# Where eight modulation columns of the hybrid block's gate are worked out: five at the end of the first branch, three later

## The chip, the cores and the metric

The kernel runs on one core of a Trainium2 chip. The metric is the time of one execution on the device in microseconds (us), as the median of several executions. A core has five engines with a queue each: TensorE (PE) for matmuls, with its weight loads shown apart (PEld), VectorE (DVE) and ScalarE (ACT) for elementwise work, GpSimd (POOL), and SyncE (SP), which here issues the large transfers from memory. Each engine works its own instructions off in the order in which they were written into its queue, and waits at an instruction until the results that it needs are there.

## What is computed

Two layers work on 256 tokens of width 1024. Each layer has three branches in a row: a gated feed-forward branch, a mixer and another feed-forward branch. In layer 0 the mixer is a hybrid (a recurrence and a state-space part), in layer 1 an mLSTM. So there are six branches, numbered 0 to 5 below; branch 0 is the first feed-forward branch, branch 1 the hybrid. Each branch is modulated by a vector `c`, by three sets of 1024 numbers: a shift, a scale and a gate.

```python
mod = (c_act @ ada_w[layer] + ada_b[layer]).reshape(bsz, N_SUB, 3, D_MODEL)[:, :, :, None, :]

def modulate(t, sub):
    return rms_norm(t, norm_g[layer, sub]) * (1.0 + mod[:, sub, 1]) + mod[:, sub, 0]

h = modulate(x, 0)
x = x + HALF_STEP * (1.0 + mod[:, 0, 2]) * swiglu(h, ffn_w_gate[layer, 0], ffn_w_up[layer, 0], ffn_w_down[layer, 0])
h = modulate(x, 1)
...
x = x + (1.0 + mod[:, 1, 2]) * y.astype(x.dtype)
```

The change is about `mod[:, 1, 2]` of layer 0, the gate of the hybrid: it is needed only when the hybrid's output projection ends.

## The kernel before

**Layout.** Features lie on the 128 partitions, tokens along the row. `x` is 8 chunks of 128 by 256. A weight matrix is cut into tiles of 128 by 128, and all tiles of the program stand in one stream in memory in the order of their use. Eight tiles are a piece (512 KB); there are 366 pieces, 66 of them in branch 0 (pieces 0 to 65) and 54 in branch 1 (pieces 66 to 119). Products are made in a split form: a weight and an activation are each a high part and a low part, and one tile costs three matmuls (L372 high by high, L373 high by low, L374 low by high).

**A piece on its way.** SP issues its transfer into `wraw` (four buffers, L91), ACT makes the high part `whi` (L99), DVE the low part `wlo` (L100). Four buffers mean that the transfer of piece n+4 waits for the low part of piece n. The parts have six buffers.

**The modulation.** A branch needs 24 columns of 128 numbers: 8 of shift, 8 of scale, 8 of gate. One column is one job: a transfer of 512 KB (L228, three buffers, on SP's queue among the pieces) and one DVE instruction that multiplies by `c` and sums (L230, tile `ada`). A table says at which pieces the jobs of a range are issued, in equal steps:

```python
for s, (lo, hi), jobs in ADA_PLAN:
    for i, b in enumerate(jobs):
        due.setdefault(starts[s] + lo + (hi - lo) * i // len(jobs), []).append(b)
```

Job b belongs to branch b // 24; jobs 40 to 47 are the gate of the hybrid, 48 to 63 shift and scale of branch 2. A planner in the framework then works out, from its own costs, in what order each engine's instructions stand; so a change of the table also moves other instructions of DVE, ACT, PE and SP against each other.

**From branch 0 to branch 1.** Branch 0 ends with its down projection: eight outputs `od` of 22 tiles. After each, DVE adds it to `x` (L492), ACT squares it (L349), DVE sums the squares (L353) and ACT and DVE make a scaled copy `hb` (L418, L419). `begin` (L422) starts branch 1: PE multiplies the first four output tiles `bc` with these copies, which don't need the norm yet. Meanwhile PE sums the squares over the partitions (`rst_n`, L317), DVE works the reciprocal root out in eight dependent instructions on 128 by 2 numbers (L329, then L283 to L292, tiles `rsv_n`, `rsy_n`, `rsw_n`), PE spreads it (`rsb_n`, L340), ACT copies it (`rs`, L427), and then each of the 8 chunks gets its normed input: a product `ht` (L402, DVE), its high part (L404, ACT) and its low part (L405, DVE, written into `hb`). After that the four `bc` are finished (`bct`, L451, and `shc_bc`, L453, DVE).

**The hybrid's first products.** `xbc` 0 to 7 are eight outputs of one piece each, with `dtT` (24 small matmuls) among them. They stand in four PSUM banks that are used in turn, so `xbc4` takes the bank of `xbc0`. A bank comes free when its convolution has read it: one ACT instruction (L619) and three DVE instructions (L622, on 255, 254 and 253 columns). The four `bc` go through twelve such L622 too (`ssd`).

**Later in the hybrid** come the products `xl`, `z` and `ri` with the recurrence's elementwise work, then the state-space part: ACT makes exponentials `mt` (L875), DVE masks them (L877), PE multiplies (`y`, L897); after that the output projection, whose inputs `ysb` are split on ACT and DVE (L359, L360).

Of the kernel before, what the change touches and what calls it, by code (L numbers as in the profile page):

```python
# [37 lines left out]
for _n, _w in COLS:  # L38
# [25 lines left out]


ADA_PLAN = [
    (0, (17, 43), range(16, 40)), (0, (43, 65), range(48, 64)), (1, (22, 37), range(40, 48)),
    (2, (6, 60), range(64, 104)), (3, (6, 60), range(104, 136)), (5, (6, 40), range(136, 144)),
]

# [1348 lines left out]
```

## Time and profile before

| | |
|---|---|
| median of 3 executions | 1103.49 us (1103.45 to 1104.76) |
| the profiled execution | 1104.36 us, of which the span of its instructions is 1102.6 us |
| PE busy | 1088.9 us (99%) |
| DVE busy | 920.0 us (83%) |
| ACT busy | 641.7 us (58%) |
| memory read | 269.77 MB, 246 GB/s over the span |

Times in the profile are us from the start of the span. A row of the timeline has the start, the duration, the engine, the line, the operation, what it writes and reads, the shape, how many equal ones follow each other, and in brackets how long the engine sat idle before it and who ended that. Matmuls overlap each other: each is shown as 0.28 us long, but the next starts 0.113 us later when nothing is in the way, so a gap between two starts tells of a wait even where PE counts as busy. Two DVE instructions overlap as well, by about 0.08 us.

### The profile page before, as it was taken

What the parts mean: (1) busy time and instruction counts of PE and PEld (TensorE: products, weight loads), DVE (VectorE), ACT (ScalarE), POOL (GpSimd) and SP (SyncE); (2) the same over time, 40 slices, a digit from 0 to 9 for tenths busy, and PEclk for the clock granted to TensorE, in tenths of its full rate; (3) what the DMA queues carried; (4) which work ended last, traced back from release to release, by engine and by line L of the source; (5) the groups of instructions that cost most, each with busy time, mean ns of one, the idle gap of its engine ahead of it and who ended that gap; (6) DMA issues with size and microseconds to landing.
All of it is one profiled execution on the core that took longest, in us unless ns stands there. A gap on an engine that the chain in (4) does not pass through costs nothing.

```text
span 1102.6 us, 23366 instructions
## 1 busy us (share of the span) xinstructions
PE 1088.9 (99%) x9350; PEld 1074.5 (97%) x9350; DVE 920.0 (83%) x1651; ACT 641.7 (58%) x1051; POOL 9.4 (1%) x29
## 2 busy tenths in 40 slices
PE   8999999999999999999999999999999999999997
PEld 6999999999999999999999999999999999999997
DVE  7999989899999899989699988869778868766552
ACT  5665545578986565454554554548776655544452
POOL 0000000000000000000000000010000000000000
PEclk9999999999999999999999999999999999999999
DMA  9899999565855489999848998953422554776551
GB/s 371 333 328 372 382 343 353 185 209 182 279 167 175 144 294 371 352 354 329 281 163 317 333 331 307 312 203 116 147 94 95 200 192 161 263 238 198 193 173 39
DMA packets 74990, 272.34 MB, mean 247 GB/s; under 512 B 8417, under 2 KB 8577, under 8 KB 74882
## 3 DMA queue, kind: packets, MB, share of 16 engines
q1 hardware_dynamic: 74304, 269.49, 69.4%
q8 instruction: 73, 1.20, 0.4%
q0 software_dynamic: 432, 1.10, 0.4%
q14 instruction: 35, 0.29, 0.1%
q10 hardware_dynamic: 146, 0.27, 0.1%
HBM read 269.77 MB, written 1.05 MB: 246 GB/s over the span
## 4 chain that ended last, share of the span: by engine, by line
PE 90%; DVE 5%; ACT 2%; DMA 1%; issue 1%; SPq 0%; DVEq 0%; ACTq 0%
PE gu L373 13%; PE gu L374 13%; PE gu L372 13%; PE od L373 10%; PE od L372 10%; PE od L374 10%; DVE wlo L100 2%; PE zz L373 1%; PE zz L374 1%; PE zz L372 1%; PE gu_f L434 1%; PE gu_f L436 1%; PE gu_f L435 1%; DVE xc L622 1%; DVE ada L230 1%
## 5 line engine op out<-in xcount | busy, mean ns | idle before, releaser
L100 DVE TENSOR_TENSOR wlo<-wraw,whi 128x1024 fp32r<-128x1024 f32 x366 | 445.6, 1222 | 94.7 <-ACT whi L99 93.2
L99 ACT CAST whi<-wraw 128x1024 fp32r<-128x1024 f32 x364 | 379.5, 1050 | 222.5 <-PE od L373 70.9
L373 PE MATMUL gu<-hb,whi 128*128 128x256 f32 x1312 | 361.0, 276 | 1.3 <-DVE hb L569 1.3
L374 PE MATMUL gu<-hb,wlo 128*128 128x256 f32 x1312 | 360.6, 276 | 0.0
L372 PE MATMUL gu<-hb,whi 128*128 128x256 f32 x1312 | 357.8, 277 | 1.6 <-ACT hb L404 1.0
L373 PEld LDWEIGHTS gu<-hb,whi 128*128 128x128 f32 x1312 | 246.3, 188 | 1.9 <-DVE hb L569 1.9
L372 PEld LDWEIGHTS gu<-hb,whi 128*128 128x128 f32 x1312 | 244.2, 188 | 2.5 <-ACT hb L404 1.2
L374 PEld LDWEIGHTS gu<-hb,wlo 128*128 128x128 f32 x1312 | 246.3, 188 | 0.0
L372 PE MATMUL od<-ph,whi 128*128 128x256 f32 x704 | 194.3, 276 | 0.0
L373 PE MATMUL od<-ph,whi 128*128 128x256 f32 x704 | 194.3, 276 | 0.0
L374 PE MATMUL od<-ph,wlo 128*128 128x256 f32 x704 | 194.3, 276 | 0.0
L230 DVE SCALAR_TENSOR_TENSOR ada<-ada,cact 128x1024 f32<-128x1024 f32 x144 | 175.4, 1220 | 0.9 <-DMA ada<-in_adaT_dram 0.9
L372 PEld LDWEIGHTS od<-ph,whi 128*128 128x128 f32 x704 | 132.2, 188 | 0.0
L373 PEld LDWEIGHTS od<-ph,whi 128*128 128x128 f32 x704 | 132.2, 188 | 0.0
L374 PEld LDWEIGHTS od<-ph,wlo 128*128 128x128 f32 x704 | 132.2, 188 | 0.0
L359 ACT CAST ph<-fg 128x256 fp32r<-128x256 f32 x88 | 35.4, 410 | 102.0 <-DVE fg L516 101.9
L360 DVE TENSOR_TENSOR ph<-fg,ph 128x256 fp32r<-128x256 f32 x88 | 36.7, 423 | 12.3 <-ACT ph L359 12.1
L492 DVE SCALAR_TENSOR_TENSOR x<-od,gate,x 128x256 f32<-128x256 f32 x48 | 23.1, 482 | 27.5 <-PE od L374 27.5
L349 ACT ACTIVATE sq_o<-x 128x256 f32<-128x256 f32 x42 | 17.6, 419 | 41.7 <-DVE x L492 37.6
L373 PE MATMUL zz<-hb,whi 128*128 128x256 f32 x128 | 36.3, 284 | 0.0
L372 PE MATMUL zz<-hb,whi 128*128 128x256 f32 x128 | 36.2, 283 | 0.0
L374 PE MATMUL zz<-hb,wlo 128*128 128x256 f32 x128 | 36.2, 283 | 0.0
(412 smaller groups left out, 1953.2 us busy)
## 6 DMA issues: line engine op xcount, KB each, us to landing
wraw<-in_wst_dram SPq DMA_DIRECT2D x366, 512.0 KB, 4.6
ada<-in_adaT_dram SPq DMA_DIRECT2D x144, 512.0 KB, 5.6
xn<-in_x_dram SPq DMA_DIRECT2D x2, 512.0 KB, 4.1
wgr<-in_ml_wg_dram POOLq DMA_DIRECT2D x3, 256.0 KB, 3.0
out_dram<-res SPq DMA_DIRECT2D x3, 256.0 KB, 2.4
out_dram<-res ACTq DMA_DIRECT2D x1, 256.0 KB, 2.8
cols<-in_cols_dram SPq DMA_DIRECT2D x1, 226.0 KB, 7.3
wkr<-in_ml_wkr_dram POOLq DMA_DIRECT2D x1, 128.0 KB, 2.3
```

The lines of the kernel that those rows point to most:

```text
L99: raw_hi = nc.scalar.copy(hi, raw)
L100: self.last = nc.vector.tensor_tensor(out=lo, in0=raw, in1=hi.bitcast(F32), op=ALU.subtract)
L230: return nc.vector.scalar_tensor_tensor(out=raw, in0=raw, scalar=1.0, in1=cact, op0=ALU.mult, op1=ALU.mult, accum_out=mods[s][:, m:m + 1])
L349: square = nc.scalar.activation(q, x, AF.Square).ins
L359: nc.scalar.copy(hi, src)
L360: nc.vector.tensor_tensor(out=both[:, 1, :], in0=src, in1=hi.bitcast(F32), op=ALU.subtract)
L372: m = nc.tensor.matmul(dst, wh, both[:, 0, :], start=start, stop=False, skip_group_check=True)
L373: nc.tensor.matmul(dst, wh, both[:, 1, :], start=False, stop=False, skip_group_check=True)
L374: nc.tensor.matmul(dst, wl, both[:, 0, :], start=False, stop=stop, skip_group_check=True)
L434: nc.tensor.matmul(dst, wh, rh, start=(k == 0), stop=False)
L435: nc.tensor.matmul(dst, wh, rl, start=False, stop=False)
L492: nc.vector.scalar_tensor_tensor(out=xs_t[d], in0=dst, scalar=g[:, d:d + 1], in1=xs_t[d], op0=ALU.mult, op1=ALU.add)
```

## The change

Only the table changes. Jobs 40 to 44, five columns of the hybrid's gate, are issued after jobs 48 to 63 in branch 0, over pieces 43 to 65, where 16 jobs stood over pieces 43 to 64; so there are 21 jobs over 23 pieces. Jobs 45 to 47 are issued in the hybrid over 12 pieces (24 to 35), where eight jobs stood over 15 (22 to 36). Nothing is added to the work and nothing is taken from it.

```diff
@@ -64,7 +64,7 @@
 ADA_PLAN = [
-    (0, (17, 43), range(16, 40)), (0, (43, 65), range(48, 64)), (1, (22, 37), range(40, 48)),
+    (0, (17, 43), range(16, 40)), (0, (43, 66), [*range(48, 64), *range(40, 45)]), (1, (24, 36), range(45, 48)),
     (2, (6, 60), range(64, 104)), (3, (6, 60), range(104, 136)), (5, (6, 40), range(136, 144)),
 ]
```

The planner orders the engines' queues anew. Three places of DVE's queue follow. The first is where branch 0 ends: the last addition to `x` (`od_7`) and the start of the reciprocal root. Before:

```order
L492 SCALAR_TENSOR_TENSOR x<-od_7_2555,gate_1962,x 128x256
L720 TENSOR_SCALAR dt<-cols 128x8
L329 TENSOR_SCALAR rsv_n_2667<-rst_n_2662 128x2
L419 SCALAR_TENSOR_TENSOR hb<-x,scale_1968,hb 128x256
L283 TENSOR_SCALAR rsy_n_2670<-rsv_n_2667 128x2
```

And now:

```order
L492 SCALAR_TENSOR_TENSOR x<-od_7_2567,gate_1965,x 128x256
L720 TENSOR_SCALAR dt<-cols 128x8
L100 TENSOR_TENSOR wlo_2549<-wraw_2546,whi_2548 128x1024
L230 SCALAR_TENSOR_TENSOR ada_2552,mod_1184<-ada_2552,cact 128x1024
L419 SCALAR_TENSOR_TENSOR hb<-x,scale_1971,hb 128x256
L329 TENSOR_SCALAR rsv_n_2682<-rst_n_2677 128x2
```

The low part of piece 67 and one of the moved columns now stand between the last addition and the root. The second place follows at once: the rest of the root, up to the first normed chunk `ht_0`. Before:

```order
L286 TENSOR_TENSOR rsw_n_2669<-rsy_n_2670 128x2
L287 SCALAR_TENSOR_TENSOR rsw_n_2669<-rsw_n_2669,rsv_n_2667 128x2
L288 SCALAR_TENSOR_TENSOR rsw_n_2669<-rsw_n_2669 128x2
L289 SCALAR_TENSOR_TENSOR rsy_n_2670<-rsw_n_2669,rsy_n_2670 128x2
L290 TENSOR_TENSOR rsw_n_2669<-rsy_n_2670 128x2
L291 SCALAR_TENSOR_TENSOR rsw_n_2669<-rsw_n_2669,rsv_n_2667 128x2
L292 SCALAR_TENSOR_TENSOR rsy_n_2670<-rsw_n_2669,rsy_n_2670 128x2
L100 TENSOR_TENSOR wlo_2690<-wraw_2687,whi_2689 128x1024
L402 SCALAR_TENSOR_TENSOR ht_0_2807<-x,scale_1968,rs_2661 128x256
```

And now:

```order
L286 TENSOR_TENSOR rsw_n_2684<-rsy_n_2685 128x2
L100 TENSOR_TENSOR wlo_2589<-wraw_2586,whi_2588 128x1024
L230 SCALAR_TENSOR_TENSOR ada_2592,mod_1184<-ada_2592,cact 128x1024
L287 SCALAR_TENSOR_TENSOR rsw_n_2684<-rsw_n_2684,rsv_n_2682 128x2
L288 SCALAR_TENSOR_TENSOR rsw_n_2684<-rsw_n_2684 128x2
L289 SCALAR_TENSOR_TENSOR rsy_n_2685<-rsw_n_2684,rsy_n_2685 128x2
L290 TENSOR_TENSOR rsw_n_2684<-rsy_n_2685 128x2
L291 SCALAR_TENSOR_TENSOR rsw_n_2684<-rsw_n_2684,rsv_n_2682 128x2
L292 SCALAR_TENSOR_TENSOR rsy_n_2685<-rsw_n_2684,rsy_n_2685 128x2
L100 TENSOR_TENSOR wlo_2622<-wraw_2619,whi_2621 128x1024
L100 TENSOR_TENSOR wlo_2705<-wraw_2702,whi_2704 128x1024
L402 SCALAR_TENSOR_TENSOR ht_0_2822<-x,scale_1971,rs_2676 128x256
```

The low part of piece 68 and the last of the five moved columns stand inside the root, and the low parts of pieces 69 and 70 behind it; before, only that of piece 70 stood there, and those of 67 to 69 ahead of the last addition. From `ht_0` to the convolutions of `xbc0` the same instructions stand in another order (the four `bct` come earlier, the first `bct` behind `ht_1`). On PE, `dtT` now stands among the products of `xbc0` and `xbc1`, and the spread of the root ten tiles later; between `xbc3` and `xbc4` nothing was put. The third place is in the state-space part, ahead of the first mask `mt` (L877). Before:

```order
L100 TENSOR_TENSOR wlo_4090<-wraw_4087,whi_4089 128x1024
L819 SCALAR_TENSOR_TENSOR lru_aq<-a_7_4012,lru_aq 128x256
L230 SCALAR_TENSOR_TENSOR ada_4093,mod_1184<-ada_4093,cact 128x1024
L939 TENSOR_SCALAR lru_aq<-lru_aq 128x1024
L881 TENSOR_TENSOR ce_4022<-ce_4022,ssd_2656 128x512
L939 TENSOR_SCALAR lru_aq<-lru_aq 128x1024
L877 TENSOR_TENSOR mt_4021<-mt_4021,cbt 128x1024
```

And now:

```order
L100 TENSOR_TENSOR wlo_4096<-wraw_4093,whi_4095 128x1024
L812 SCALAR_TENSOR_TENSOR lru_x<-thi_4013,lru_x 128x256
L819 SCALAR_TENSOR_TENSOR lru_aq<-a_7_4018,lru_aq 128x256
L939 TENSOR_SCALAR lru_aq<-lru_aq 128x1024
L881 TENSOR_TENSOR ce_4028<-ce_4028,ssd_2671 128x512
L877 TENSOR_TENSOR mt_4027<-mt_4027,cbt 128x1024
```

Of six columns that stood ahead of this mask in the hybrid, two are left; a third stands behind it.

## The prediction

> **What bounds the kernel now.** I read the page's engine shares first, then the engines by stretch, the waits of PE, and last the timelines of DVE, PE and ACT where the change moves things.
>
> ```profile
> span 1102.6 us, 23366 instructions
> PE 1088.9 (99%) x9350; PEld 1074.5 (97%) x9350; DVE 920.0 (83%) x1651; ACT 641.7 (58%) x1051; POOL 9.4 (1%) x29
> ```
>
> PE is taken 99% of the time, so the kernel is as long as PE's queue plus the stalls inside it. A stall can hide under that 99%, because each matmul is shown longer than the distance to the next. The stretches tell more:
>
> ```profile
> core 0: us, PE busy (x) PEld busy (x) DVE busy (x) ACT busy (x) POOL busy (x), PEclk, DMA share, GB/s
> 57.00:136.00 79.00, 79.00 (x700) 79.00 (x699) 76.22 (x127) 44.61 (x72) 0.00 (x0) 1.00 0.97 362
> 136.00:197.00 61.00, 61.00 (x541) 61.00 (x540) 55.28 (x85) 30.31 (x40) 0.99 (x3) 1.00 0.92 334
> 197.00:210.00 13.00, 13.00 (x107) 12.72 (x107) 10.40 (x29) 5.07 (x11) 0.00 (x0) 1.00 0.63 234
> 210.00:237.00 27.00, 27.00 (x237) 26.91 (x236) 26.90 (x54) 23.04 (x41) 0.00 (x0) 1.00 0.58 194
> 237.00:299.00 62.00, 61.51 (x523) 60.09 (x521) 61.37 (x126) 53.09 (x108) 0.00 (x0) 1.00 0.69 225
> ```
>
> The down projection of branch 0 runs from 136 to 197: 541 matmuls in 61.00 us, 0.113 us each, no stall. DVE has 5.7 us to spare there. From 210 on, the hybrid, DVE has nothing to spare: 26.90 of 27.00 and 61.37 of 62.00 us. PE lives there on low parts made ahead and on free banks. The waits that the profile puts down to DVE or ACT in the hybrid are short:
>
> ```profile
> PE y L897 <- DVE mt L877: 0.4, 1, 0.4
> PE od L373 <- DVE ysb L360: 0.3, 1, 0.3
> ```
>
> So relief of DVE inside the hybrid can win little, and lateness of DVE on entering it can cost, if PE has no slack where it first needs DVE. It has none at `xbc4`, which needs the bank of `xbc0`:
>
> ```profile
> 223.57 0.28 PE L373 MATMUL xbc<-hb,whi 128*128 128x256 f32 x1
> 223.69 0.28 PE L374 MATMUL xbc<-hb,wlo 128*128 128x256 f32 x1
> 223.88 0.36 PE L372 MATMUL xbc<-hb,whi 128*128 128x256 f32 x1
> ...
> 214.70 4.81 DVE L622 SCALAR_TENSOR_TENSOR ssd<-bct,cols,ssd 128x255 f32<-128x255 f32 x12
> 219.43 2.35 DVE L100 TENSOR_TENSOR wlo<-wraw,whi 128x1024 fp32r<-128x1024 f32 x2
> 221.70 2.42 DVE L622 SCALAR_TENSOR_TENSOR ssd_x<-xbc,cols,ssd_x 128x255 f32<-128x255 f32 x6
> 224.04 1.22 DVE L100 TENSOR_TENSOR wlo<-wraw,whi 128x1024 fp32r<-128x1024 f32 x1
> ```
>
> The six convolutions of `xbc0` and `xbc1` start every (224.04 - 221.70)/6 = 0.39 us and take turns, so the last of `xbc0` is the fifth: 221.70 + 5 x 0.39 = 223.65, some 0.1 later with its tail. PE ends `xbc3` with the matmul at 223.69, could go on at 223.80 and goes on at 223.88. PE and DVE arrive together; what makes DVE later here, PE waits for in full.
>
> **The moved columns and branch 0.** Five jobs go from the hybrid to pieces 43 to 65. By number they cost branch 0 five transfers of 512 KB and five DVE sums. I cost the transfers at nothing: 24 jobs over 26 pieces (0.92 a piece) run in pieces 17 to 42 of the same branch, the stretch 57 to 136, at 0.113 us a matmul (700 in 79.00 us), and 21 over 23 is 0.91. The cover is the low parts made ahead; without it a transfer late by one place would cost PE one transfer's time, 512 KB at the 362 GB/s of that stretch, 1.4 us. Of the five sums, three fall before the last addition to `x` (19 where 16 were) and two behind it. The low parts of pieces 67, 68 and 69 move from before it to behind it. A sum takes 1.15 us of queue and a low part 1.14:
>
> ```profile
> 190.93 1.22 DVE L230 SCALAR_TENSOR_TENSOR ada<-ada,cact 128x1024 f32<-128x1024 f32 x1
> ...
> 192.08 0.42 DVE L353 TENSOR_TENSOR ssq<-ssq,sq_o 128x256 f32<-128x256 f32 x1
> ...
> 196.80 0.48 DVE L492 SCALAR_TENSOR_TENSOR x<-od,gate,x 128x256 f32<-128x256 f32 x1 [1.35 <-PE od L374]
> 197.20 0.16 DVE L720 TENSOR_SCALAR dt<-cols 128x8 f32<-128x8 f32 x1
> 198.94 0.16 DVE L329 TENSOR_SCALAR rsv_n<-rst_n 128x2 f32<-128x2 f32 x1 [1.58 <-PE rst_n L317]
> 199.03 0.48 DVE L419 SCALAR_TENSOR_TENSOR hb<-x,scale,hb 128x256 fp32r<-128x256 f32 x1
> 199.43 0.16 DVE L283 TENSOR_SCALAR rsy_n<-rsv_n 128x2 int32<-128x2 int32 x1
> 199.63 0.16 DVE L286 TENSOR_TENSOR rsw_n<-rsy_n 128x2 f32<-128x2 f32 x1
> ...
> 200.88 1.22 DVE L100 TENSOR_TENSOR wlo<-wraw,whi 128x1024 fp32r<-128x1024 f32 x1
> 202.17 0.88 DVE L402 SCALAR_TENSOR_TENSOR ht<-x,scale,rs 128x256 f32<-128x256 f32 x2
> ```
>
> (From 190.93 to 192.08 the sum; two low parts in 221.70 - 219.43 = 2.27.) Three sums in, three low parts out: DVE's load before the addition stays level, and it waited 1.35 us there, so the addition still starts at 196.80, when PE is through.
>
> **Behind it the queue is longer, and that is the main term.** From 196.80, with these prices, as the rows now stand: addition 0.40, `dt` 0.08, low part 67 and a sum 2.29, `hb` 0.40; that is 199.97, past the 198.94 at which the root could start. Three small steps 0.48 (0.20 for one that needs the one before, 0.08 for one that doesn't), low part 68 and the last moved sum 2.29, six small steps 1.08, low parts 69 and 70 2.27: `ht_0` starts at 206.09, where it was 202.17. The spread of the root on PE, ten tiles later now, is due at about 201.0 + 10.7 x 3 x 0.12 = 204.9 and holds nothing up.
>
> From `ht_0` to the end of `xbc0`'s convolutions, the same instructions as before in new order: 16 of `ht` and `hb` at 0.40, 6.4; four `bct` at 0.33 and four copies at 0.07, 1.6 (rows below); five low parts, 5.68; twelve convolutions of `bct`, 219.43 - 214.70 = 4.73; five of `xbc`, 1.95. Sum 20.36, so 226.45 with no wait at all. There is one: the first `bct` now stands behind `ht_1`, where DVE arrives at 206.89, and its bank is finished only when 6 of 32 tiles of `bc` remain:
>
> ```profile
> 209.55 0.42 DVE L451 TENSOR_TENSOR bct<-bc,rs 128x256 f32<-128x256 f32 x1
> 209.88 0.47 DVE L402 SCALAR_TENSOR_TENSOR ht<-x,scale,rs 128x256 f32<-128x256 f32 x1
> 210.28 0.15 DVE L453 COPY shc_bc<-bc 128x1 f32<-128x1 f32 x1
> 210.35 0.41 DVE L451 TENSOR_TENSOR bct<-bc,rs 128x256 f32<-128x256 f32 x1
> ...
> 209.81 0.28 PE L436 MATMUL bc<-hb,wlo 128*128 128x258 f32 x1
> 209.92 0.28 PE L372 MATMUL xbc<-hb,whi 128*128 128x256 f32 x1
> ```
>
> Nineteen matmuls of 0.12 before 209.92 its last one starts, 207.6, and ends 0.28 later: 207.9, a wait of 1.0 us. That gives 227.5 for the bank, against 223.7. Lower bound of the stall: 226.45 + 0.1 - 223.80 = 2.7 us. Upper: 227.5 and the 0.7 us that DVE waited for ACT among its `hb` before, 4.4. I take 227.5: a stall of **3.7 us at `xbc4`**. Behind the waiting matmul stands all of PE's queue. Two cushions that could hide it are used up: `dtT`, 24 matmuls or 2.9 us, was moved forward into `xbc0` and `xbc1`, where the late chunks would otherwise stall PE, and between `xbc3` and `xbc4` nothing stands.
>
> **What the hybrid gives back.** Later five sums less stand on DVE, 5.75 us; worth what PE waited for DVE. At the first mask:
>
> ```profile
> 298.36 0.28 PE L373 MATMUL gl<-hb,whi 128*128 128x256 f32 x1
> 299.06 0.33 PE L897 MATMUL y<-mt,ssd 128*64 128x128 f32 x2 [0.42 <-DVE mt L877]
> ...
> 296.23 1.14 ACT L875 ACTIVATE mt<-mt 128x1024 f32<-128x1024 f32 x1
> ...
> 324.24 0.39 PE L372 MATMUL od<-ysb,whi 128*128 128x256 f32 x2
> 324.94 0.39 PE L373 MATMUL od<-ysb,whi 128*128 128x256 f32 x1 [0.31 <-DVE ysb L360]
> ```
>
> From 298.36 to 299.06 PE lost 0.58. DVE comes four sums earlier now, 4.6 us, but ACT ends its exponential at 297.37, and a mask of 1.2 us after that leaves 298.7: 0.36 back. At 324.24, two matmuls would end their turns at 324.47; 0.47 lost, and two sums less and a low part less stand ahead, so it comes back. Together 0.8; bounds 0 and 1.05. I take 0.6, since masks of the next pairs move later by some tenths. With 3.7 that is **+3.1 us** on the span. The profiled execution was 1104.36 us around a span of 1102.6, 0.87 over the median of 1103.49; the difference goes on the median: **1106.6 us**.
>
> **Rivals.** First, a smaller stall: the lower bound 2.7 and all of 1.05 given back make +1.65, 1105.1 us. For it speaks that the waits of DVE on ACT vanish where `bct` now fill them; against, that `bct` itself must wait for PE.
>
> Second, the relief pays in full and it is not slower. In 237 to 299 a matmul takes 62.00/523 = 0.1185 us, 0.0055 more than in the stretch without stalls, 2.9 us in all. If a full DVE causes that, freeing it from the start of that stretch wins up to 2.9, and 0.8 of the waits: 3.7 against 3.7, 1103.5 us, and faster wherever the stall is under 3.5. Against: the profile names only 0.4 and 0.3 us of waits, and small products of other kinds stand in the stretch.
>
> Third, the stall lets PE's clock fall. The row at the end of the program shows that it does after a pause:
>
> ```profile
> 1088.00:1095.50 7.50, 7.50 (x70) 7.50 (x69) 0.48 (x1) 0.93 (x2) 0.00 (x0) 1.00 0.00 0
> 1099.00:1102.60 3.60, 0.00 (x0) 0.00 (x0) 0.00 (x0) 0.00 (x0) 0.00 (x0) 0.54 0.60 226
> ```
>
> PE's last matmuls end around 1096, and the mean granted clock of the last 3.6 us is 0.54. A stall of 3.7 us is about that long. As long again at half clock would lose half of it, 1.9 us: 1108.5 us. [...]
>
> Fourth, the transfers in branch 0 are late after all and PE stalls before 197: two late ones, 2.8 us, 1109.4.
>
> **How the numbers follow.** A measurement here tells 0.2%, 2.2 us, from no change. Forecast 0.56; smaller stall 0.17; relief in full 0.12; clock 0.08; late transfers 0.07. Slower by over 0.2%: forecast, clock and transfers, less 0.04 at the forecast's edge, 0.67. Within 0.2%: the smaller stall, half of the second rival and that edge, 0.27. Faster: the other half, 0.06. The forecast's own range is 1104.8 (2.7 less 1.05, and its edge) to 1107.9 (4.4, nothing back); with the rivals 1103.0 to 1109.0 leaves out about 2 in 10.
>
> **What would show it.** Right: `ht_0` near 206, six convolutions of `xbc` starting near 225.5, and a gap between two `xbc` matmuls near 223.8 of 2.7 to 4.4 us with a convolution L622 as its end; matmuls 0.113 apart until 197; the waits at `y` and `od` shorter. Wrong: no gap there, `ht_0` before 205, gaps in branch 0, or a clock below 1 after the stall.

## The result

The changed kernel takes 1111.08 us (median of 4 executions, 1110.61 to 1112.27) against 1103.79 us: a ratio of 1.0066, with a 95% interval of 1.0054 to 1.0078. That is 7.3 us slower. The prediction said slower too, but by 3.1 us, and 1111.08 lies outside its range of 1103.0 to 1109.0.

The head of the page of the changed kernel, in answer to the first rows shown of before:

```profile
span 1108.9 us, 23372 instructions
PE 1090.5 (98%) x9350; PEld 1076.9 (97%) x9350; DVE 920.8 (83%) x1651; ACT 642.1 (58%) x1051; POOL 9.4 (1%) x29
```

The work is the same, 9350 matmuls, and the span is 6.3 us longer. The engines by stretch and the waits of PE (engine, line, who was waited for: us in total, times, longest) say where to look:

```profile
136.00:197.00 61.00, 61.00 (x540) 61.00 (x538) 55.60 (x88) 27.91 (x38) 0.98 (x3) 1.00 0.96 355
210.00:237.00 27.00, 23.59 (x191) 23.36 (x190) 27.00 (x53) 21.81 (x39) 0.00 (x0) 0.94 0.64 218
237.00:299.00 62.00, 62.00 (x532) 60.98 (x531) 58.50 (x123) 51.99 (x101) 0.00 (x0) 1.00 0.62 200
...
PE xbc L372 <- DVE ssd_x L622: 3.4, 1, 3.4
PE rst_n L317 <- ACT sq_o L349: 1.1, 1, 1.1
PE od L373 <- DVE ysb L360: 0.6, 1, 0.6
PE y L897 <- DVE mt L877: 0.5, 1, 0.5
PE rst_g L317 <- DVE gacc L911: 0.5, 2, 0.3
```

Until 197 PE keeps its pace (540 matmuls in 61.00 us). From 210 to 237 it does 191 where it did 237, DVE is full, and the clock column, which was 1.00, reads 0.94. The wait at `xbc4` is new. The waits at `y` and `od`, which were to shrink, are 0.5 and 0.6 us where they were 0.4 and 0.3. And there is a wait that the prediction did not speak of, `rst_n`, the sum of squares with which branch 2 starts: 1.1 us, where before it was 0.27.

The timelines of PE and DVE around the wait at `xbc4`:

```profile
223.13 0.38 PE L714 MATMUL dt<-ident,dtt 128*128 128x128 f32 x2
226.92 0.38 PE L372 MATMUL xbc<-hb,whi 128*128 128x256 f32 x1 [3.41 <-DVE ssd_x L622]
...
228.18 0.33 PE L373 MATMUL xbc<-hb,whi 128*128 128x256 f32 x1
228.31 0.42 PE L374 MATMUL xbc<-hb,wlo 128*128 128x256 f32 x1
228.52 0.42 PE L372 MATMUL xbc<-hb,whi 128*128 128x256 f32 x1
...
205.40 0.88 DVE L402 SCALAR_TENSOR_TENSOR ht<-x,scale,rs 128x256 f32<-128x256 f32 x2
207.17 0.42 DVE L451 TENSOR_TENSOR bct<-bc,rs 128x256 f32<-128x256 f32 x1 [0.89 <-PE bc L436]
224.83 2.42 DVE L622 SCALAR_TENSOR_TENSOR ssd_x<-xbc,cols,ssd_x 128x255 f32<-128x255 f32 x6
```

The last addition to `x` came 0.62 us earlier in this execution than in that of before (196.18 and 196.80), so 0.62 is added for a comparison: `ht_0` at 206.02 (forecast 206.09), the wait for the first `bct` 0.89 us (forecast 1.0), the convolutions of `xbc` at 225.45 (forecast near 225.5). PE waits 3.41 us behind two transposes `dt`. Counted as the forecast does, from 223.13, where `xbc4` could have gone on, to 226.92, PE is 3.79 us late. But 1.4 us after it has gone on, at 228.3, the matmuls are suddenly 0.21 us apart instead of 0.113. Cut into stretches of 3.41 us, which is how long the clock stays at 0.50 at either place below, with the granted clock in the third column from the end:

```profile
221.44:224.85 3.41, 2.07 (x19) 1.83 (x17) 3.41 (x7) 3.41 (x7) 0.00 (x0) 1.00 0.33 115
224.85:228.27 3.42, 1.35 (x11) 1.35 (x12) 3.42 (x8) 2.22 (x5) 0.00 (x0) 1.00 0.75 254
228.27:231.68 3.41, 3.41 (x18) 3.41 (x17) 3.41 (x8) 1.55 (x3) 0.00 (x0) 0.50 0.61 175
375.04:378.45 3.41, 2.32 (x20) 2.11 (x19) 1.76 (x6) 1.25 (x4) 1.06 (x2) 1.00 0.55 157
378.45:381.87 3.42, 3.42 (x18) 3.42 (x17) 2.52 (x10) 0.00 (x0) 0.00 (x0) 0.50 0.02 7
```

For one such stretch the clock is halved, 18 matmuls are done where there is room for about 30 at 0.113 us each, and then it is whole again. The same happens once more at 378, behind the wait of 1.1 us at `rst_n`. From 228.27 to 378.45 are 150.18 us, 44.0 times the 3.41.

To see where each run gains and loses, the start of the same matmul (the n-th of its name) is compared with the trace of before, and the change of that difference is taken by place. These are the columns used below, in us: xbc4 (218 to 234 in the time of before, the stall and what follows it), hybrid (234 to 347), and branch 2 (347 to 389, the start of branch 2).

| | xbc4 | hybrid | branch 2 |
|---|---|---|---|
| the change | +5.4 | -0.5 | +2.1 |

Of the 5.4, 3.8 are there when PE goes on and 1.6 come with the half clock. The rest of the program is the same to 0.1 us, but for a start that was 0.6 us earlier in this execution. Each figure compares one execution with one execution. The profiled one of the changed kernel is the fastest of its four (1110.61 us), and that of before is 0.6 us over its median.

In the eleven traces here the mean granted clock of the execution is 0.998 or 0.999 without a halved stretch ahead of the program's end, 0.997 with one and 0.995 with two. An estimate from that for executions without a trace: two of the four executions of the change had one halved stretch (0.997) and two had at least two (0.995 and 0.994).

### The profile page after: what moved, and what is told of

The parts are those of the page before. It is cut to its first block, busy times and chain, and to the rows that moved or that the text cites. A ratio compares the mean times of both kernels' runs of the same rounds, so it can differ in the third digit from the quotient of the medians.

```text
span 1108.9 us, 23372 instructions
## 1 busy us (share of the span) xinstructions
PE 1090.5 (98%) x9350; PEld 1076.9 (97%) x9350; DVE 920.8 (83%) x1651; ACT 642.1 (58%) x1051; POOL 9.4 (1%) x29
## 4 chain that ended last, share of the span: by engine, by line
PE 84%; DVE 9%; ACT 4%; issue 2%; DMA 1%; SPq 0%; DVEq 0%; ACTq 0%
PE gu L373 13%; PE gu L374 13%; PE gu L372 12%; PE od L372 9%; PE od L373 9%; PE od L374 9%; DVE wlo L100 2%; PE zz L373 1%; PE zz L374 1%; PE zz L372 1%; ACT whi L99 1%; PE gu_f L434 1%; PE gu_f L435 1%; PE gu_f L436 1%; DVE ada L230 1%
```

## The experiments

The theory after the result: the stall at `xbc4` is understood; the half clock behind it, and the start of branch 2, are not. And it was open whether the relief of the hybrid is worth anything. All runs below were timed in five rounds beside the kernel before, but for the second trace of the changed kernel. Lines left out of a diff are marked by three dots.

### The five columns left out

```diff
-(0, (43, 66), [*range(48, 64), *range(40, 45)]), (1, (24, 36), range(45, 48)),
+(0, (43, 65), range(48, 64)), (1, (24, 36), range(45, 48)),
+            if s == 1:
+                nc.gpsimd.memset(mods[s][:, 16:21], 0.0)
```

> The five moved columns are left out of the program altogether (their five gate columns stay zero); the hybrid keeps its three, branch 0 is as before. So this is the relief of DVE in the hybrid without any burden at the boundary. By the prediction's term it gives 0.6 us (0 to 1.05): 1102.4 to 1103.8 us, no change that can be measured, and the waits at y and od shrink. By the rival 'relief in full' it gives 3.7 us: about 1100.1 us. A third theory, from the trace of the changed kernel, where DVE waits for PE and ACT in the state-space part: the freed 5.75 us of DVE turn into waits of DVE there, and the time moves by less than 0.5 us. No stall of PE at xbc4 by any of them.

Measured: 1105.2 us, ratio 1.0012 (1.0004 to 1.0021). With five transfers and five sums less to do, the program is not faster; by the interval it is a little slower. By place: xbc4 +0.1, hybrid -0.2, branch 2 +0.5. The trace is of the fastest of eleven executions (1104.08 us) and has no halved stretch. Five of the eleven have a granted clock of 0.997, and these are the slowest (1105.43 to 1106.55 us). Of the theories only the third fits up to 347; none had the loss at branch 2. DVE's own waits in the state-space part show where its free time went:

```profile
DVE rsv_g L331 <- PE rst_g L319: 2.4, 2, 1.2
DVE wlo L100 <- ACT whi L99: 2.1, 4, 0.8
DVE lru_aq L821 <- ACT a L820: 1.0, 1, 1.0
```

With smaller ones DVE waits 7.4 us here (290 to 356 us) for PE and ACT; before, it waited 1.9 us in the same stretch, and for PE's sums of squares (`rst_g`) not at all.

### The transfers alone, and the sums alone

In the first, the five columns are transferred in branch 0 and not summed; in the second, five sums are made on data that is already there.

```diff
...
+        if 40 <= b < 45:
+            return
```

> The change, but the five moved columns are only transferred, never multiplied and summed (their gate columns stay zero). Theory T, the transfers: they use up the lead of the weights at the end of branch 0, so three low parts (3.4 us) still fall behind the last addition; less what DVE waited there before, PE stalls 1.5 to 2.5 us at xbc4, and the low part of piece 67 ends 2 to 4 us ahead of its use where it was 9.8. Theory S, the sums on DVE (the prediction took the transfers at nothing): no stall at xbc4 over 0.5 us, the lead of piece 67 stays over 8 us.

```diff
+        if 40 <= b < 45:
+            return nc.vector.scalar_tensor_tensor(out=raw, in0=cact, scalar=1.0, in1=cact, ...)
...
         nc.sync.dma_start(raw, a["adaT"][b])
```

> The change, but the five moved columns' instructions work on data that is already there: five sums on DVE at the same places, no transfer (the five gate columns are wrong). Theory T: all five sums find room ahead of the last addition, the low parts stay where they were, the stall at xbc4 is 0 to 1.2 us, and the time lies between 1102.5 and 1105. Theory S: DVE's 5.75 us come through to the boundary, the stall at xbc4 is 2.7 to 4.4 us and the time is 1106 or more.

Measured: transfers alone 1108.46 us, ratio 1.0037 (1.0024 to 1.0049); sums alone 1111.67 us, ratio 1.0072 (1.0059 to 1.0084). The first row is PE's at `xbc4` with the transfers alone; the others are of the sums alone: PE's last matmul of branch 0, DVE's last addition to `x`, PE's sum of squares that waits for it, the stretch behind that with half clock, and the wait at `xbc4`.

```profile
225.94 0.38 PE L376 MATMUL xbc<-hb,whi 128*128 128x256 f32 x1 [1.74 <-DVE ssd_x L626]
```

```profile
196.50 0.28 PE L377 MATMUL od<-ph,wlo 128*128 128x256 f32 x1
202.95 0.48 DVE L495 SCALAR_TENSOR_TENSOR x<-od,gate,x 128x256 f32<-128x256 f32 x1
203.93 0.61 PE L320 MATMUL rst_n<-ones,sq_o 128*128 128x1 f32 x4 [1.38 <-ACT sq_o L352]
...
204.84:208.26 3.42, 3.42 (x18) 3.42 (x18) 2.91 (x11) 0.00 (x0) 0.00 (x0) 0.50 0.98 381
...
PE xbc L375 <- DVE ssd_x L625: 2.9, 1, 2.9
```

Theory T was right about the transfers (a stall of 1.74 us, where 1.5 to 2.5 were expected) and wrong about the sums; theory S was right about the sums and wrong about the transfers. The sums alone make a stall of 2.9 us at `xbc4`. Before it, PE waits 1.4 us at the root and a stretch of half clock follows (0.50 from 204.84 to 208.26), so that PE is 3.1 us late there, because the planner put all five ahead of the last addition, which starts 6.2 us after PE is through. The transfers alone lose 2.1 us more where branch 2 starts, with a halved stretch there too (0.50 from 376.34 to 379.76). Neither half is free. DVE had 5.72 us to spare in this stretch (61.00 less 55.28), and five sums are 5.75 us. So "it is the transfers" falls, and so does "it is the sums": the reserve at the end of branch 0, weights made ready ahead of their use, is drawn down by either. Before, the low part of piece 67 was begun at 189.80 and used 11 us later (200.77); in the changed kernel it was begun at 196.65 and used 3.6 us later (200.26).

### The pause filled

```diff
...
+                if i == 4:
+                    fill = ax_bank("fill", "q")
+                    fills = [nc.tensor.matmul(fill[:, 0:T], dt_parts[0][:, 0:P], h[0][:, 0, :], start=True, stop=True)
+                             for _ in range(28)]
+                    in_one_go(fills, [m])
                 m = project(b[:, 0:T], h)
...
```

> The change, with 28 matmuls that nobody reads put on PE between xbc3 and xbc4, some 3.2 us of work inside the stall of 3.6 us. The bank comes when DVE's convolution has read it, so the wait ends at the same time. Theory C, the clock falls after a stretch with too little work: no half clock between 224 and 236, matmuls of xbc4 0.113 to 0.12 us apart throughout, 1.6 us faster than the changed kernel, about 1109.5 us. Rival: the slow matmuls behind the stall have another cause than the pause; then they stay 0.21 us apart for 3.4 us and the time stays at 1111.

Measured: 1110.7 us, ratio 1.0063 (1.0049 to 1.0077). Theory C is right at the place, its rival falls, and its time is missed. The filler, and the engines around it:

```profile
223.92 3.48 PE L703 MATMUL fill<-hb,wdh 128*128 128x256 f32 x28
227.24 0.38 PE L725 MATMUL dt<-ident,dtt 128*128 128x128 f32 x2
...
216.00:240.00 24.00, 23.91 (x206) 23.68 (x205) 24.00 (x44) 19.45 (x32) 0.00 (x0) 1.00 0.63 205
373.91:377.33 3.42, 1.79 (x16) 1.58 (x15) 2.31 (x6) 2.33 (x6) 1.06 (x2) 1.00 0.75 234
377.33:380.74 3.41, 3.41 (x17) 3.41 (x18) 1.99 (x11) 0.00 (x0) 0.00 (x0) 0.50 0.04 14
380.74:384.15 3.41, 3.41 (x18) 3.41 (x18) 1.44 (x3) 0.37 (x1) 0.00 (x0) 0.50 0.39 132
```

The clock stays at 1.00 from 216 to 240, and xbc4 costs +4.0 instead of +5.4. But PE, earlier by that much, waits longer where branch 2 starts (1.6 us at `rst_n`, where it was 1.1), and there the clock is now halved for two stretches: branch 2 +4.2 instead of +2.1. In this execution, what was won at one pause was lost at the next. It is the slowest of the five (1112.68 us, granted clock 0.995); the fastest, with 0.998, took 1110.27 us, so the filler won no more than about 0.8 us against the changed kernel even where no stretch was halved.

### Both pauses filled

The same 28, and ten more ahead of `rst_n` at the start of branch 2, behind the first three tiles of `gu_f`:

```diff
+            if nm == "n2":
+                fills = [nc.tensor.matmul(pt[:, T:2 * T], dt_parts[0][:, 0:P], h[0][:, 0, :], start=True, stop=True)
+                         for _ in range(10)]
...
```

> The change, with 28 unread matmuls in the stall at xbc4 and 10 more (1.1 us) ahead of the sum of squares where branch 2 starts, the second place where PE waited (1.1 us) and the clock fell behind it. Theory C, the clock falls after a stretch with too little work: no half clock between 200 and 1090, 1.6 and 1.3 us less than the changed kernel, of which up to 0.5 is lost again where PE then waits longer for DVE: 1108.2 to 1108.8 us. Rival D, the end of the hybrid is set by DVE, and a PE that comes there earlier only waits longer: the time stays over 1110 us.

Measured: 1110.0 us, ratio 1.0053 (1.0040 to 1.0065).

```profile
216.00:240.00 24.00, 23.91 (x206) 23.67 (x204) 24.00 (x43) 18.56 (x32) 0.00 (x0) 1.00 0.61 202
370.00:384.00 14.00, 13.82 (x117) 13.41 (x116) 12.14 (x31) 7.13 (x16) 1.06 (x2) 1.00 0.51 172
```

No half clock at either place now (0.999 in all five executions, 1109.21 to 1110.40 us), and the time falls between the two expectations: 1.1 us less than the changed kernel, not 2.3 to 2.9. By place: xbc4 +4.0, hybrid +0.1, branch 2 +1.1. So the kernel is still about 6 us slower than before without any halved stretch, and by this run the clock is the smaller part of the loss. The hybrid gave back nothing here, where it gave 0.5 in the changed kernel; the filler also moved instructions of DVE, and which of them it was is open.

### The changed kernel again

> The changed kernel once more, for a second trace: the same queues. The stall at xbc4 is 3.4 to 3.8 us again and the wait where branch 2 starts 1.0 to 1.5 us. If the half clock depends on how the stall falls into stretches of 3.41 us that run on regardless of the program, the places where the clock is halved may differ (at 224 to 232, at 376 to 384, at both or at none), and the time by 1.3 to 1.6 us for each. If it depends on the length of the stall alone, the half clock comes at the same two places.

Measured: 1110.42 us, one execution. By place: xbc4 +5.5, hybrid -0.6, branch 2 +0.9.

```profile
225.06:228.48 3.42, 0.77 (x6) 0.77 (x7) 3.42 (x9) 2.34 (x5) 0.00 (x0) 1.00 0.81 266
228.48:231.89 3.41, 3.41 (x18) 3.41 (x17) 3.41 (x7) 1.51 (x3) 0.00 (x0) 0.50 0.47 167
375.25:378.66 3.41, 2.26 (x21) 2.05 (x19) 2.01 (x5) 2.01 (x6) 1.06 (x2) 1.00 0.62 217
378.66:382.07 3.41, 3.41 (x29) 3.26 (x29) 2.79 (x11) 0.23 (x1) 0.00 (x0) 1.00 0.04 12
```

The same queues and nearly the same waits (1.15 us at `rst_n`, 1.09 in the first trace), and this time no half clock at 378. So the length of a wait doesn't decide alone. The busy time of PE in the stretch (2.32 us before the half clock, 2.26 here) hardly tells the two cases apart either. That it matters how the wait falls into the stretches is the expectation that is left; no run moved a wait to show it. The 1.2 us between branch 2 in the two traces (+2.1 and +0.9) is the price there.

### The columns done twice, and the places of the other three

Three runs ask what the hybrid's half of the change is worth. In the first, branch 0 works as in the change and the hybrid keeps all eight columns at their old places:

```diff
-(1, (24, 36), range(45, 48)),
+(1, (22, 37), range(40, 48)),
```

> The change, but the hybrid keeps all its eight columns at their old places, so that five are worked out twice: the burden of branch 0 without any relief of the hybrid. Theory H, the relief is hidden behind other waits of the state-space part: 1110.5 to 1112 us, as the changed kernel. If the relief pays 0.6 us as in the prediction: 1111.7 us; if it pays 2 us or more under the delay that the changed kernel has: over 1113 us. A stall of 3.4 to 3.8 us at xbc4 by all of them.

In the second the five are left out, as in the first run of all, but the other three stand where they stood before:

```diff
-(1, (24, 36), range(45, 48)),
+(1, (22, 37), [None] * 5 + list(range(45, 48))),
```

> The five columns left out, as in the run without them, but the other three stay at the places in the hybrid that they had before (pieces 31, 33 and 35 instead of 24, 28 and 32). Theory H, the relief is hidden by the chain of exponential, mask, product and root in the state-space part: 1103.3 to 1104.8 us, no change. Theory O, the relief is real but the new order of DVE's queue that came with the new places spends it: faster than before by 0.6 to 3.7 us, 1100.4 to 1103.5 us.

In the third nothing is left out: this second edit alone is made to the changed kernel.

> The change with only its first half: five columns in branch 0, but the other three at the places that they had before (pieces 31, 33 and 35). Theory O, the new places of the three cost something of their own (the two runs without the five columns differ by 1.7 us in this alone, 1105.2 and 1103.5): no wait over 0.6 us where branch 2 starts, no half clock there, 1108.0 to 1109.8 us. Rival: the wait where branch 2 starts comes from the lateness at the hybrid's entry, whatever the places; then it stays at 1.0 to 1.5 us and the time at 1110.4 to 1111.5 us. The stall at xbc4 is 3.4 to 3.8 us by both.

| | us | ratio (95% interval) | xbc4 | hybrid | branch 2 |
|---|---|---|---|---|---|
| the change | 1111.08 | 1.0066 (1.0054 to 1.0078) | +5.4 | -0.5 | +2.1 |
| five done twice, eight in the hybrid | 1109.05 | 1.0043 (1.0031 to 1.0056) | +5.3 | -1.3 | -0.2 |
| the change, three at old places | 1108.79 | 1.0041 (1.0027 to 1.0055) | +6.3 | -1.1 | -0.2 |
| five left out, three at new places | 1105.2 | 1.0012 (1.0004 to 1.0021) | +0.1 | -0.2 | +0.5 |
| five left out, three at old places | 1103.48 | 0.9997 (0.9988 to 1.0006) | +0.4 | -1.1 | -0.1 |

The run with more work in the hybrid, the columns done twice, is the faster one by 2.0 us, outside all that was expected of it. The reason is in the last column: at the old places nothing is lost where branch 2 starts. The new places of three columns, pieces 24, 28 and 32 instead of 31, 33 and 35, make the planner order the hybrid anew, and that order costs 1.7 us without the five columns (1105.2 and 1103.5) and 2.3 us with them (1111.1 and 1108.8, where a second stretch of half clock at xbc4 even speaks against the latter). The last run came out as its theory O expected: no wait and no half clock where branch 2 starts, though the lateness at the hybrid's entry is the same. Part of the 1.7 us is the clock: of the eleven executions at the old places none has a granted clock under 0.998, at the new places five have. The waits of PE with the five left out, first at the new places, then at the old:

```profile
PE rst_n L319 <- ACT sq_o L351: 0.8, 1, 0.8
PE od L375 <- DVE ysb L362: 0.6, 1, 0.6
PE y L899 <- DVE mt L879: 0.6, 1, 0.6
PE rst_g L319 <- DVE gacc L913: 0.5, 2, 0.3
```

```profile
PE rsb_g L343 <- DVE rsy_g L295: 0.6, 1, 0.6
PE y L900 <- DVE mt L880: 0.5, 1, 0.5
PE rst_n L320 <- ACT sq_o L352: 0.2, 1, 0.2
```

And with the new order DVE starts the second root later, having waited for PE's sums; at the old places it doesn't wait there:

```profile
329.57 0.16 DVE L331 TENSOR_SCALAR rsv_g<-rst_g 128x2 f32<-128x2 f32 x1 [1.21 <-PE rst_g L319]
```

```profile
326.61 0.16 DVE L332 TENSOR_SCALAR rsv_g<-rst_g 128x2 f32<-128x2 f32 x1
```

Three microseconds between the two starts, for the same work. Theory O holds for the loss at branch 2. In the hybrid the old places give 1.1 instead of 0.2, but that needs no relief: the columns done twice, with all eight sums in the hybrid, give 1.3 there. What gives it is open, and 0.6 us of it can lie in the one execution of before that all are compared with. Theory O's price for the relief, faster by 0.6 to 3.7, doesn't hold: even at the old places the time is the same as before (0.9988 to 1.0006), so theory H, a hidden relief, stands for that. The run with the change's first half shows the stall at `xbc4` of 3.4 us by itself, and how the half clock can come earlier and last longer:

```profile
222.04:225.46 3.42, 1.40 (x13) 1.16 (x11) 3.42 (x6) 3.29 (x6) 0.00 (x0) 1.00 0.48 171
225.46:228.87 3.41, 2.02 (x9) 2.02 (x10) 3.41 (x8) 1.67 (x3) 0.00 (x0) 0.50 0.48 167
228.87:232.28 3.41, 3.41 (x18) 3.41 (x17) 3.41 (x6) 1.47 (x2) 0.00 (x0) 0.50 0.62 215
```

No run beats the kernel before. The one at par leaves five columns out, so in the two orders tried there is nothing that can be measured (0.12% at most) for this knob to win in the hybrid.

## Why the prediction was right and wrong

Two terms stood at nothing in the sum, and these are the steps that failed: the half clock behind the stall, which measured 1.6 us, and the start of branch 2, which measured 2.1 us in the first trace and 0.9 in the second. The other parts come first.

**What bounds the kernel, and the place of the stall: right.** PE's queue and its stalls set the time, and the new stall stood at `xbc4`, with the convolution L622 at its end.

**The walk through DVE's queue: right to 0.1 us.** `ht_0`, the wait of the first `bct` and the start of the convolutions are compared above. `xbc4` went on 3.79 us late, against 3.7. The profile's wait is shorter, 3.41 us, because "between `xbc3` and `xbc4` nothing stands" was wrong, and so is the same remark in the section on the change: two transposes `dt` stood there (223.13 to 223.51), which before ran at 234.8.

**"I cost the transfers at nothing": right only until 197.** No matmul of branch 0 came late. But the transfers alone stall PE 1.74 us after it, by the reserve of low parts that they use up. The sum held all the same, since the walk had the low parts of pieces 67 to 69 behind the last addition by their order, whatever had put them there.

**The give-back of 0.6 us: right in size by luck, wrong in reason.** The hybrid gave 0.5 to 0.6 back in both traces. But the waits at `y` and `od`, from which it was worked out, did not shrink. With DVE relieved and no delay at the entry it gives 0.2 at the new places, and with the delay and no relief 1.3 at the old. So it comes without a relief too; what gives it is not shown.

**The clock: here it failed.** The prediction named a clock below 1 after the stall as a sign of being wrong, and that came. It made the half clock a rival of 0.08, and no run shows a reason for so low a chance. The pause that it had for comparison, at the program's end, has no matmul in its last 3.6 us. The rows show that the clock also falls with matmuls in the stretch: in each of the four traces with a stall of 3.4 us at `xbc4` and no filler in it (the change twice, the columns done twice, the first half) the clock was halved to 0.50 behind it, after stretches of 3.41 us with 11, 6, 8 and 13 matmuls in them. The price was as the rival had it: 1.6 us forecast as about 1.9. The prediction held the right price and the wrong chance.

**The start of branch 2: not seen at all.** The sum ended with the hybrid's products. There DVE is late once more: its last addition to `x` starts 1.41 us after PE's last product of the hybrid (375.94 and 374.53), where it was 0.58 (370.93 and 370.35). PE waits 1.1 us at `rst_n`, and a second half clock can follow: +0.9 or +2.1 us. The step that should have found it is "later five sums less stand on DVE", which priced the relief by what PE had waited before, as if the rest of the queue stayed as it was. It doesn't: the three columns left were placed anew as well, and the order that the planner made of that puts DVE's roots behind PE's sums. That the places make the loss is shown by the runs at the old ones; the steps from the late roots to the late last addition were not followed.

**The rivals.** The smaller stall and the late transfers did not come; "the relief pays in full" is refuted by the run at the old places; the clock came. In the profiled execution: 3.8 at `xbc4`, 1.6 by the clock, -0.5 in the hybrid, 2.1 at branch 2, together 7.0, of which 0.6 is set against the earlier start of this execution; the two spans differ by 6.3 and the medians by 7.3. The missing 1.0 us has no trace, since the profiled execution is the fastest of its four and that of before lies over its median. The forecast had 3.7 and -0.6.

## What to carry to other kernels

Before work is moved into a stretch without stalls, look at the reserve with which that stretch hands over to the next one, not only at its busy time: a stall can come later, at the first place where the other engine is needed at once. A stall of PE is to be priced both ways, with half clock behind it and without: here half clock came after waits of 1.09 to 1.6 and of 3.4 us, and not after 1.15, 1.74 and 2.9. A filler shows what of the loss is the clock's. Where a planner orders the queues, the relieved side must be read in the new order too; price a relief by leaving the work out before paying for its move.

## What the runs showed of the hardware that was not expected

Behind the stalls the half clock lasted one stretch of 3.41 us or two, without an idle one ahead of it (the one with the least work had PE busy 0.77 us). For the pause at `xbc4` the rows above and those of other runs order themselves by how long PE was busy in the stretch. The clock was halved after stretches with PE busy 0.77 us (6 matmuls, the second trace of the change), 0.97 (8, the columns done twice), 1.35 (11, the first trace of the change) and 1.40 (13, the first half). It stayed whole after 2.07 (19, the first trace) and after these two, the first with the transfers alone, the second with the sums alone:

```profile
222.74:226.16 3.42, 1.68 (x14) 1.44 (x14) 3.42 (x8) 2.51 (x4) 0.00 (x0) 1.00 0.60 184
226.16:229.57 3.41, 3.41 (x32) 3.41 (x32) 3.41 (x6) 2.81 (x5) 0.00 (x0) 1.00 0.63 210
```

```profile
228.74:232.15 3.41, 1.88 (x15) 1.88 (x16) 3.41 (x8) 1.71 (x4) 0.00 (x0) 1.00 0.54 185
```

What the clock does after 1.40 to 1.68 us of work no run shows. And the order doesn't hold at other places: where branch 2 starts, the clock fell after 2.32 us (the first trace) and 2.34 (the transfers alone) and held after 2.26 (the second trace), and at the first root with the sums alone it fell after 2.03. What decides between these cases was not tested by a run.
